# An encoder layer on one core: first loads in another order and smaller pieces, five tiles projected unscaled, a tied operand in the gate/up stage, and the last tile in two column halves

## The chip, the core and the metric

The kernel runs on one core of a Trainium2 chip. Its engines are TensorE (PE; weight loads are listed apart as PEld), VectorE (DVE), ScalarE (ACT), GpSimd (POOL) and SyncE (SP), which issues most loads. The metric is the device time of one execution in microseconds.

## What is computed

One encoder layer over 1280 tokens (a prompt of 256 and a sample of 1024) of width 1024, in float32:

```python
def encoder_layer(x, ...):
    h = rmsnorm(x, attn_norm_g)
    proj = h @ w_in                     # 384 q latents, 256 kv latents, 32 rotary, 3*512 for NA
    a = mla_group(proj[..., :o1], proj[..., o1:o2], proj[..., o2:o3], ...)
    b = na_group(proj[..., o3:], na_rpb)
    mix = jnp.concatenate([rmsnorm(a, mla_out_g), rmsnorm(b, na_out_g)], axis=-1)
    x = x + mix @ w_o
    h2 = rmsnorm(x, ffn_norm_g)
    x = x + (jax.nn.silu(h2 @ w_gate) * (h2 @ w_up)) @ w_down
    return x
# then y = rmsnorm(x, final_norm_g)
```

`mla_group` normalises the latents, rotates the 32 rotary columns and attends over all tokens; `na_group` attends over a window of the token grid.

## The kernel before, in words

**Products.** Every operand is split into a high part (a cast to fp32r) and a low part (the difference); `mm3` (L108) makes three matmuls, L110 to L112, for each 128-row slice: high times high, high times low, low times high. ACT makes the casts; DVE or POOL makes the differences. The tokens are ten tiles of 128 (`NT`), the width eight slices of 128 (`KC`).

**Order.** Tile, the framework, puts every engine's instructions in order with a planner that simulates a timeline and prefers what stands earlier in the program; SP alone keeps the program's order (`manual_schedule`). `tc.issue_after(ins)` puts what is traced inside behind `ins` on its engine. A tile of a pool with `bufs=n` waits until the tile n allocations earlier was used for the last time.

**Latents (L120 to L296).** `w_c` (1024 x 672) is loaded in eight slices, `load_wc` (L138), and scaled by the gain when it is split (`split_g`). x comes twice: transposed as `x_T`, for the products, and by tokens as `x_tm`, for the sum of squares (`rms_x`, L158: a Square on ACT, then two steps on POOL, `rstd_of`). For the first `NU` = 3 tiles x is split as it is loaded, in halves of four slices, between the weight slices; their latents are scaled by the row's factor when they leave PSUM, and x is scaled and split again afterwards (`scale_x`, L167), since the later products read the scaled x in `hT_h`, `hT_l`. `scale_x` spreads the factor to a 128 x 128 tile `r_m` on POOL, lays it across by a product `rr` on PE (bank from the pool `px`), multiplies on DVE (L173) and splits (L152, L153). For tiles 3 to 9 `norm_tile` (L176) does all this ahead of the latents, traced three tiles ahead.

`latents(t)` (L182) sums two PSUM banks `lat` (384 and 288 columns, four banks in rotation) over the eight slices, takes them out (L198 to L203), normalises, and transposes them in two groups through the bank `trc` (L223, L226, L227) into `stg`. `rope_q(t)` multiplies `stg` by `wr` into the bank `pr` (loaded by `load_wr` in three pieces through the buffers of the last weight slices), rotates, and transposes again (L260). In between PE has the first q and k products for the neighbourhood attention, `qk_ftile` (L310), in column chunks of 256, 512 and 512; `HOLD` (L130) puts a chunk behind a step of a tile: step 0 and 1 are the two transpose groups, 2 the rope transposes. Then V is projected with `w_v`, whose buffers lie where the latent stage's were.

**Gate/up (L898 to L1077).** The two FFN input products are made by a scheme of seven sub-products `m` for each pair of 128-column weight blocks; S[m] is an activation operand (sums of quarters `R["11"]` to `R["22"]`), `operand(A, m)` (L892) forms the weight operand: block sums on POOL (`sum_A`, L890), then a cast on ACT (L879) and a difference on POOL (L880) into the ring `wc` of six. For the first pair (`fp` = 0) the order is written out: products 1 and 2 of gate and of up, then 6, 7, 4, 5, 3. Product 6 is the third. Its S6 is built in five token slices from `T2[0..4]`, some of which lie in the buffers `sum` and `A21` that the sums of `operand(.., 6)` need. `differences` (L860) finishes R["12"] and R["21"] for the last two tiles on DVE.

**Down and tail (L1081 to L1233).** The second FFN product is again seven sub-products over eleven steps; m = 7 is last, and its last five steps are made tile by tile for five tiles. After each tile `put` adds PSUM to x (L1143), `final_half` (L1164) takes the Square of the left 512 columns, adds the right half's sum (`prepare`, made earlier), forms the factor in three POOL steps (L1170, L89, L91), scales the left half on DVE and the right half on ACT, and stores both.

## Time and profile before

| | us |
|---|---|
| median of 3 runs | 1632.9 (1630.91 to 1635.21) |
| the profiled execution, its own time | 1632.26 |
| its span | 1630.4 |
| PE busy in it | 1589.9 (98%) |
| DVE, ACT, POOL busy | 884.4 (54%), 715.6 (44%), 663.0 (41%) |
| mean granted clock of TensorE | 0.992 |

Line numbers are those of the kernel before. A group of instructions or a wait is given with the engine, the line and "written tile <- read tiles". "PEclk" or clock is the share of full speed that TensorE was granted: 1.00 is 2.4 GHz, 0.50 is 1.2 GHz. Matmuls are pipelined, so a record's duration is longer than the distance from one start to the next.

### The profile page before, as it was taken

What the parts mean: (1) busy time and instruction counts of PE and PEld (TensorE: products, weight loads), DVE (VectorE), ACT (ScalarE), POOL (GpSimd) and SP (SyncE); (2) the same over time, 40 slices, a digit from 0 to 9 for tenths busy, and PEclk for the clock granted to TensorE, in tenths of its full rate; (3) what the DMA queues carried; (4) which work ended last, traced back from release to release, by engine and by line L of the source; (5) the groups of instructions that cost most, each with busy time, mean ns of one, the idle gap of its engine ahead of it and who ended that gap; (6) DMA issues with size and microseconds to landing.
All of it is one profiled execution on the core that took longest, in us unless ns stands there. A gap on an engine that the chain in (4) does not pass through costs nothing.

```text
span 1630.4 us, 25683 instructions
## 1 busy us (share of the span) xinstructions
PE 1589.9 (98%) x9601; PEld 1447.9 (89%) x9601; DVE 884.4 (54%) x1473; ACT 715.6 (44%) x1478; POOL 663.0 (41%) x823
## 2 busy tenths in 40 slices
PE   7998999999999999999989999999999999999998
PEld 7997889998888888888889999999999998888886
DVE  4654035456777777533374444344444346886676
ACT  5534145455677777644353222333232233443334
POOL 3451425544111119324677656656655651010002
PEclk9999999999999999999999999999999999999999
DMA  6635312234001021234312332222322237843434
GB/s 220 215 101 150 61 39 51 48 107 163 21 18 35 21 94 33 69 108 151 136 33 92 105 109 67 77 94 90 109 99 77 77 120 264 298 140 96 155 102 153
DMA packets 123244, 171.10 MB, mean 105 GB/s; under 512 B 35504, under 2 KB 67120, under 8 KB 123120
## 3 DMA queue, kind: packets, MB, share of 16 engines
q1 hardware_dynamic: 78880, 120.30, 24.1%
q10 hardware_dynamic: 43680, 46.87, 8.3%
q0 software_dynamic: 560, 2.29, 0.3%
q8 instruction: 75, 1.23, 0.3%
q14 instruction: 49, 0.40, 0.1%
HBM read 118.96 MB, written 50.46 MB: 104 GB/s over the span
## 4 chain that ended last, share of the span: by engine, by line
PE 89%; issue 2%; DMA 2%; POOL 2%; ACT 2%; DVE 2%; SPq 0%; ACTq 0%; POOLq 0%; DVEq 0%
PE M L112 11%; PE M L110 11%; PE M L111 11%; PE d L112 5%; PE d L111 5%; PE d L110 5%; PE o L698 4%; PE tp L688 3%; PE po L110 2%; PE po L111 2%; PE pj L110 2%; PE po L112 2%; PE pj L112 2%; PE pj L111 2%; PE na_o L469 2%
## 5 line engine op out<-in xcount | busy, mean ns | idle before, releaser
L111 PE MATMUL M<-S,wc 128*128 128x320 f32 x1056 | 324.3, 309 | 0.0
L110 PE MATMUL M<-S,wc 128*128 128x320 f32 x1056 | 321.9, 309 | 0.0
L112 PE MATMUL M<-S,wc 128*128 128x320 f32 x1056 | 313.0, 310 | 4.1 <-POOL wc L880 4.1
L112 PEld LDWEIGHTS M<-S,wc 128*128 128x128 f32 x1056 | 195.4, 188 | 4.6 <-POOL wc L880 4.6
L111 PEld LDWEIGHTS M<-S,wc 128*128 128x128 f32 x1056 | 198.7, 188 | 0.0
L110 PEld LDWEIGHTS M<-S,wc 128*128 128x128 f32 x1056 | 197.9, 188 | 0.8 <-ACT wc L879 0.3
L880 POOL TENSOR_TENSOR wc<-A,wc 128x512 fp32r<-128x512 f32 x86 | 120.9, 1408 | 83.9 <-ACT wc L879 83.8
L962 DVE TENSOR_TENSOR z<-M,z 128x320 f32<-128x320 f32 x120 | 56.9, 488 | 134.2 <-PE M L112 121.7
L879 ACT CAST wc<-A 128x512 fp32r<-128x512 f32 x86 | 53.5, 622 | 162.2 <-PE M L111 146.3
L880 POOL TENSOR_TENSOR wc<-sum,wc 128x512 fp32r<-128x512 f32 x62 | 88.8, 1433 | 85.5 <-ACT wc L879 81.3
L111 PE MATMUL d<-S,S 128*128 128x512 f32 x310 | 120.7, 390 | 0.0
L112 PE MATMUL d<-S,S 128*128 128x512 f32 x310 | 120.2, 390 | 0.0
L110 PE MATMUL d<-S,S 128*128 128x512 f32 x310 | 119.9, 389 | 0.0
L962 DVE TENSOR_TENSOR zB<-M,zB 128x320 f32<-128x320 f32 x100 | 47.6, 488 | 132.8 <-PE M L112 111.0
L100 DVE TENSOR_TENSOR PT<-tp,PT 128x512 fp32r<-128x512 f32 (+1 forms) x144 | 93.0, 658 | 38.6 <-ACT PT L99 37.5
L879 ACT CAST wc<-sum 128x512 fp32r<-128x512 f32 x62 | 38.4, 619 | 144.4 <-PE M L111 99.1
L99 ACT CAST PT<-tp 128x512 fp32r<-128x512 f32 (+1 forms) x144 | 79.3, 565 | 38.3 <-PE tp L688 34.8
L680 DVE TENSOR_REDUCE mm<-S 128x1 f32<-128x1024 f32 (+1 forms) x80 | 84.8, 1061 | 10.9 <-PE S L112 9.3
L1006 ACT CAST S<-as 128x640 fp32r<-128x640 f32 x58 | 42.3, 729 | 94.4 <-issue 58.6
L682 ACT ACTIVATE ex<-S,mm 128x1024 f32<-128x1024 f32 (+1 forms) x80 | 79.7, 996 | 8.3 <-DVE mm L680 7.7
L711 POOL TENSOR_TENSOR ob<-ob 128x128 f32<-128x128 f32 x40 | 18.3, 457 | 156.9 <-ACT ob L708 153.7
L698 PE MATMUL o<-PT,v 128*128 128x256 f32 x544 | 80.6, 287 | 1.0 <-ACT PT L99 1.0
(404 smaller groups left out, 4113.3 us busy)
## 6 DMA issues: line engine op xcount, KB each, us to landing
as<-act_d SPq DMA_DIRECT2D x73, 320.0 KB
w<-in_w_down_dram SPq DMA_DIRECT2D x44, 256.0 KB
act_d<-z ACTq DMA_DIRECT2D x35, 320.0 KB
act_d<-zB ACTq DMA_DIRECT2D x35, 320.0 KB
A<-in_w_gate_dram SPq DMA_DIRECT2D x42, 256.0 KB
A<-in_w_up_dram SPq DMA_DIRECT2D x42, 256.0 KB
x<-in_x_tm_dram SPq DMA_DIRECT2D x20, 512.0 KB
cT_d<-stg ACTq DMA_DIRECT2D x20, 320.0 KB
```

The lines of the kernel that those rows point to most:

```text
L99: i = nc.scalar.copy(out=hi, in_=ps)
L100: nc.vector.tensor_sub(out=lo, in0=ps, in1=hi)
L110: nc.tensor.matmul(out, lhsT=sh, rhs=mh, start=first, stop=False, **kw)
L111: nc.tensor.matmul(out, lhsT=sh, rhs=ml, start=False, stop=False, **kw)
L112: return nc.tensor.matmul(out, lhsT=sl, rhs=mh, start=False, stop=last, **kw).ins
L680: nc.vector.reduce_max(out=nm[:, u:u + 1], in_=S, axis=AX.X, negate=True)
L682: nc.scalar.activation(ex, S, AF.Exp, bias=nm[:, u:u + 1], scale=1.0, accum_out=l[:, u:u + 1])
L688: nc.tensor.transpose(tp[:, j], ex[:, kt * P:(kt + 1) * P], ident)
L698: nc.tensor.matmul(oT, lhsT=vv, rhs=pt[s][g][:, j], start=kt == 0 and s == 0, stop=kt == nkt - 1 and s == 1)
L879: i0 = nc.scalar.copy(out=hi, in_=raw)
L880: i1 = nc.gpsimd.tensor_tensor(out=lo, in0=raw, in1=hi, op=ALU.subtract)
L962: nc.vector.tensor_add(out=o, in0=ps, in1=a)
```

## The change

- First loads: the gain vector first; x of tiles 0 and 1 in pieces of two, two and four slices between the weight slices; the first weight slice in two column pieces (384, 288), each split by itself; tile 2 after all weights. The last weight slice is loaded into `wqk_raw` and not into the ring of two.
- `NU` = 5: tiles 3 and 4 are loaded, split unscaled and projected like the first three, and scaled afterwards. Tiles 5 to 9 are loaded five tiles ahead and normalised three ahead. `w_qr` comes in one load and one split. `r_m` has two buffers, `rr` one bank instead of two, and the second transpose group has a bank of its own from `px` up to tile 6; the last tile takes banks of `lat` for its transposes and its rope product. `HOLD` names other steps for three chunks.
- Gate/up, first pair: the operand of product 6 for gate is traced before product 1 of up; the last slice of S6 is built behind its cast, and what remains of `differences` behind that slice; only the difference that reads `T2[3]` stays ahead. The operand for up is tied behind the gate operand's low half.
- Tail: for the last tile the last five steps of m = 7 are made for 256 columns and then for the other 256, with an add, a Square and a POOL step for each; the mean's factor and EPS go into `prepare`, and the factor takes one POOL step less. The right half of the last but one tile follows the last tile's last Square.

```diff
@@ -126,9 +126,9 @@
     ck = ra.tile([P, NT, RD], F32, name="ck")
     sk = ra.tile([P, NT, RD], F32, name="sk")
     wr = ra.tile([P, 2, 3, 256], F32R, name="wr")
-    wc, step = [], {}
-    HOLD = {(0, 768): (7, 2), (1, 0): (8, 2), (1, 256): (9, 0), (1, 768): (9, 1)}
-    NU = 3
+    wc, step, rrs = [], {}, {}
+    HOLD = {(0, 768): (7, 2), (1, 0): (9, 0), (1, 256): (8, 2), (1, 768): (9, 2)}
+    NU = 5
 
...
     def load_wc(kc):
-        nm = ("wqk_raw", "wqk_h", "wqk_l", "wqk_h", "wqk_l")
-        raw = (rb.tile([P, KC, P], F32, name=nm[kc], bufs=1 if kc == 0 else 2)
-               .rearrange("p a b -> p (a b)")[:, 0:CW] if kc < 5 else
+        nm = {0: "wqk_raw", 1: "wqk_h", 2: "wqk_l", 3: "wqk_h", 4: "wqk_l", 7: "wqk_raw"}.get(kc)
+        raw = (rb.tile([P, KC, P], F32, name=nm, bufs=1 if nm == "wqk_raw" else 2)
+               .rearrange("p a b -> p (a b)")[:, 0:CW] if nm else
                rx.tile([P, CW], F32, name="wc_raw", bufs=2))
-        load(raw, w_c[kc])
         h = ra.tile([P, CW], F32R, name=f"wc_h{kc}")
         l = ra.tile([P, CW], F32R, name=f"wc_l{kc}")
-        split_g(h, l, raw, kc)
+        cuts = (slice(0, QR), slice(QR, CW)) if kc == 0 else (slice(0, CW),)
+        for cs in cuts:
+            load(raw[:, cs], w_c[kc][:, cs])
+        for cs in cuts:
+            split_g(h[:, cs], l[:, cs], raw[:, cs], kc)
         wc.append((h, l))
 
-    def split_x(t, xT, q=None):
-        ks = slice(0, KC) if q is None else slice(4 * q, 4 * q + 4)
+    def split_x(t, xT, ks=slice(0, KC)):
         sl = (slice(None), ks, slice(t * P, (t + 1) * P))
         nc.scalar.copy(out=hT_h[sl], in_=xT[:, ks])
         nc.vector.tensor_sub(out=hT_l[sl], in0=xT[:, ks], in1=hT_h[sl])
 
-    def load_half(t, xT, q):
-        load(xT[:, 4 * q:4 * q + 4], x_T[t, :, 4 * q:4 * q + 4])
-
-    def rms_x(t):
+    def load_part(t, a, b):
+        load(xu[t][:, a:b], x_T[t, :, a:b])
+        split_x(t, xu[t], slice(a, b))
+
+    def load_x(t):
         x = rx.tile([P, D], F32, name="x", bufs=2)
         load(x, x_tm[t * P:(t + 1) * P, :])
+        return x
+
+    def rms_x(x):
         ss = ra.tile([P, 1], F32, name="ssx", bufs=2)
         nc.scalar.activation(x, x, AF.Square, accum_out=ss)
         r = ra.tile([P, 1], F32, name="rx", bufs=4)
@@ -165,24 +171,26 @@
         return r
 
     def scale_x(t, xT, r):
-        rm = ra.tile([P, P], F32, name="r_m", bufs=1)
+        rm = ra.tile([P, P], F32, name="r_m", bufs=2)
         nc.gpsimd.tensor_scalar(out=rm, in0=ones, scalar1=r, scalar2=1.0, op0=ALU.mult,
                                 op1=ALU.mult)
-        rr = px.tile([P, P], F32, name="rr", bufs=2)
-        nc.tensor.matmul(rr, lhsT=rm, rhs=ident, start=True, stop=True)
+        rr = px.tile([P, P], F32, name="rr")
+        rrs[t] = nc.tensor.matmul(rr, lhsT=rm, rhs=ident, start=True, stop=True).ins
         nc.vector.tensor_mul(out=xT, in0=xT, in1=rr.unsqueeze(1).to_broadcast([P, KC, P]))
         split_x(t, xT)
 
-    def norm_tile(t):
-        xT = (rb.tile([P, KC, P], F32, name="wqk_h", bufs=2) if t in (3, 4) else
-              rx.tile([P, KC, P], F32, name="xT", bufs=3))
+    def load_tile(t):
+        xT = rx.tile([P, KC, P], F32, name="xT", bufs=3)
         load(xT, x_T[t])
-        scale_x(t, xT, rms_x(t))
+        return xT, load_x(t)
+
+    def norm_tile(t, xT, x):
+        scale_x(t, xT, rms_x(x))
 
     def latents(t, r0=None):
         ts_ = slice(t * P, (t + 1) * P)
-        pq = pa.tile([P, QR], F32, name="lat", bufs=4)
-        pk = pa.tile([P, QR], F32, name="lat", bufs=4)[:, 0:KVR + RD]
+        pq = pa.tile([P, 512], F32, name="lat", bufs=4)[:, 0:QR]
+        pk = pa.tile([P, 512], F32, name="lat", bufs=4)[:, 0:KVR + RD]
         for kc in range(KC):
             wh, wl = wc[kc]
             f, e = kc == 0, kc == KC - 1
@@ -218,11 +226,13 @@
                                        op0=ALU.mult, op1=ALU.mult)
         nc.gpsimd.tensor_tensor(out=kr, in0=kr, in1=t2, op=ALU.add)
         stg = ra.tile([P, 2, 6, P], F32R, name="stg", bufs=2)
-        tq = pa.tile([P, 4, P], F32, name="trc")
+        last = t == NT - 1
+        tq = pa.tile([P, 4, P], F32, name="lat" if last else "trc", bufs=4 if last else 1)
         for i in range(4):
             step[t, 0] = nc.tensor.transpose(tq[:, i], c[:, i * P:(i + 1) * P], ident).ins
         split_ps(stg[:, 0, 0:4], stg[:, 1, 0:4], tq)
-        tk = pa.tile([P, 4, P], F32, name="trc")
+        tk = (pa if t + 3 >= NT else px).tile([P, 4, P], F32, name="lat" if last else "trc",
+                                              bufs=4 if last else 1)
         nc.tensor.transpose(tk[:, 0], c[:, 4 * P:5 * P], ident)
         step[t, 1] = nc.tensor.transpose(tk[0:RD, 1], c[:, 5 * P:5 * P + RD], ident).ins
         split_ps(stg[:, 0, 4], stg[:, 1, 4], tk[:, 0])
@@ -233,14 +243,15 @@
         return stg
 
     def load_wr():
-        for c in range(3):
-            raw = rx.tile([P, CW], F32, name="wc_raw", bufs=2)[:, 0:256]
-            load(raw, w_qr[:, c])
-            split_w(wr[:, 0, c], wr[:, 1, c], raw)
+        raw = (rb.tile([P, KC, P], F32, name="wqk_raw").rearrange("p a b -> p (a b)")
+               [:, 0:768].rearrange("p (c n) -> p c n", c=3))
+        load(raw, w_qr)
+        split_w(wr[:, 0], wr[:, 1], raw)
 
     def rope_q(t, stg):
         ts_ = slice(t * P, (t + 1) * P)
-        bank = pa.tile([P, 512], F32, name="pr")
+        last = t == NT - 1
+        bank = pa.tile([P, 512], F32, name="lat" if last else "pr", bufs=4 if last else 1)
         pr = bank[:, 0:256]
         for c in range(3):
             mm3(pr, stg[:, 0, c], stg[:, 1, c], wr[:, 0, c], wr[:, 1, c], c == 0, c == 2)
@@ -263,30 +274,39 @@
         for s in range(2):
             store_r(rope_d[:, s, :, ts_].rearrange("g p t -> p g t"), sr[:, s])
 
-    xu = [rx.tile([P, KC, P], F32, name="xT", bufs=3) for _ in range(NU)]
-    load_half(0, xu[0], 0)
+    xu = [rx.tile([P, KC, P], F32, name="xT", bufs=3) for _ in range(3)]
     load(ga, g_attn)
-    split_x(0, xu[0], 0)
-    halves = [(t, q) for t in range(NU) for q in range(2)][1:]
+    load_part(0, 0, 2)
     for kc in range(KC):
         load_wc(kc)
-        if kc < len(halves):
-            t, q = halves[kc]
-            load_half(t, xu[t], q)
-            split_x(t, xu[t], q)
-    ru = [rms_x(t) for t in range(NU)]
-    norm_tile(NU)
+        for part in {0: ((1, 0, 2),), 1: ((0, 2, 4), (1, 2, 4)), 3: ((0, 4, 8), (1, 4, 8))}.get(kc, ()):
+            load_part(*part)
+    load(xu[2], x_T[2])
+    split_x(2, xu[2])
+    ru = [rms_x(load_x(0))]
     load(gq_b[:, 0:QR], g_q.partition_broadcast(P))
     load(gq_b[:, QR:], g_kv.partition_broadcast(P))
-    load(ck, cos_k)
-    load(sk, sin_k)
-    load_wr()
+    ru.append(rms_x(load_x(1)))
+    for t in (3, 4):
+        xu.append(rb.tile([P, KC, P], F32, name="wqk_h", bufs=2))
+        load(xu[t], x_T[t])
+        split_x(t, xu[t])
+        if t == 3:
+            load(ck, cos_k)
+            load(sk, sin_k)
+            ru.append(rms_x(load_x(2)))
+            load_wr()
+            ru.append(rms_x(load_x(3)))
+    ru.append(rms_x(load_x(4)))
+    ready = {}
     for t in range(NT):
-        if NU < t + 3 < NT:
-            norm_tile(t + 3)
+        if NU <= t + 3 < NT:
+            norm_tile(t + 3, *ready[t + 3])
         stg = latents(t, ru[t] if t < NU else None)
         if t < NU:
             scale_x(t, xu[t], ru[t])
+        if t + 5 < NT:
+            ready[t + 5] = load_tile(t + 5)
         if t + 3 == NT:
             rx.release()
             px.release()
@@ -995,12 +1015,15 @@
         S[m] = [pl.tile([P, 4, NQ], F32R, name=nm, bufs=2) for x in "hl"]
         cuts = [(slice(n * P, (n + 1) * P), T2[n]) for n in range(5)] if m == 6 else [
             (slice(s * NS, (s + 1) * NS), None) for s in range(2)]
-        for cs, from_ in cuts:
-            with ExitStack() as es:
-                for ins in after:
-                    es.enter_context(tc.issue_after(ins))
-                after = split_S(m, cs, from_)
+        for cs, from_ in cuts[:-1] if m == 6 else cuts:
+            after = split_after(m, cs, from_, after)
         return after
+
+    def split_after(m, cs, from_, after):
+        with ExitStack() as es:
+            for ins in after:
+                es.enter_context(tc.issue_after(ins))
+            return split_S(m, cs, from_)
...
@@ -1027,9 +1050,10 @@
             split_f(w_ring[f], raw)
             ops[5, f] = a_ring[f], w_ring[f]
 
-    with tc.issue_after(build_S(6, ())[1]):
-        for t in (NT - 2, NT - 1):
-            differences(nc.vector, t)
+    s6 = build_S(6, ())
+    with tc.issue_after(s6[1]):
+        cs8 = slice(3 * P, 4 * P)
+        difference(nc.vector, R["21"][:, :, cs8], R["21"][:, :, cs8], T2[3])
     for fp in range(NF // 2):
         zp, zn = (rB, "zB") if fp % 2 else (l4[1], "z")
         G, U = C = [zp.tile([P, 2, NTOK], F32, name=zn, bufs=2) for _ in range(2)]
@@ -1047,13 +1071,18 @@
                 if (i, m) == (1, 1):
                     w0[2, 1] = operand(A0[1], 2)
                     A0[1]["12"] = load_A(1, 0, "12", at[5])
-                if (i, m) == (1, 2):
                     w6 = [operand(A0[0], 6, at[6], "A21")]
                     hold = w6[0][2]
+                    s6 = split_after(6, slice(4 * P, 5 * P), T2[4], (hold, s6[1]))
+                    with tc.issue_after(s6[1]):
+                        difference(nc.vector, R["12"][:, :, cs8], R["22"][:, :, cs8],
+                                   R["12"][:, :, cs8])
+                        differences(nc.vector, NT - 1)
                 for s in range(2):
                     with tc.issue_after(last_mm):
                         product(C[i], w0[m, i], m, s, held[i], 0, hold)
-            w6.append(operand(A0[1], 6, at[7], "A22"))
+            with tc.issue_after(w6[0][3]):
+                w6.append(operand(A0[1], 6, at[7], "A22"))
             for n, m in enumerate(SEQ[2:]):
                 w = w6 if m == 6 else [operand(A0[i], m) for i in range(2)]
                 if m != 3:
@@ -1159,18 +1188,27 @@
     def prepare(n, junk):
         x, half = xs[n], halves[:, n:n + 1]
         nc.scalar.activation(junk, x[:, 512:], AF.Square, accum_out=half)
+        nc.vector.tensor_scalar(out=half, in0=half, scalar1=1.0 / D, scalar2=EPS,
+                                op0=ALU.mult, op1=ALU.add)
         nc.gpsimd.tensor_tensor(out=x[:, 512:], in0=x[:, 512:], in1=gl_b[:, 512:], op=ALU.mult)
 
-    def final_half(n):
+    def final_half(n, ps, cuts):
         x, half = xs[n], halves[:, n:n + 1]
         yo = l5r.tile([P, 2, 512], F32, name=f"w1_{n}").rearrange("p a b -> p (a b)")
-        ss = r5a.tile([P, 1], F32, name="ssy", bufs=3)
+        ss = r5a.tile([P, 2], F32, name="ssz", bufs=3)
         r = r5a.tile([P, 1], F32, name="ry", bufs=3)
-        nc.scalar.activation(yo[:, 0:512], x[:, 0:512], AF.Square, accum_out=ss)
-        nc.gpsimd.tensor_tensor(out=ss, in0=ss, in1=half, op=ALU.add)
-        rstd_of(r, ss, D)
+        for j, cs in enumerate(cuts):
+            nc.vector.tensor_add(out=x[:, cs], in0=ps[:, cs], in1=x[:, cs])
+            sq = nc.scalar.activation(yo[:, cs], x[:, cs], AF.Square, accum_out=ss[:, j:j + 1]).ins
+            nc.gpsimd.tensor_scalar(out=ss[:, j:j + 1], in0=ss[:, j:j + 1], scalar1=1.0 / D,
+                                    scalar2=ss[:, j - 1:j] if j else half,
+                                    op0=ALU.mult, op1=ALU.add)
+        nc.gpsimd.tensor_tensor(out=r, in0=ss[:, j:j + 1], in1=mhalf[:, 0:1], op=ALU.pow)
         nc.vector.scalar_tensor_tensor(out=yo[:, 0:512], in0=x[:, 0:512], scalar=r,
                                        in1=gl_b[:, 0:512], op0=ALU.mult, op1=ALU.mult)
+        return sq, (n, yo, x, r)
+
+    def right_half(n, yo, x, r):
         nc.scalar.activation(yo[:, 512:], x[:, 512:], AF.Copy, scale=r)
         load(y[n * P:(n + 1) * P, 0:512], yo[:, 0:512])
         store(y[n * P:(n + 1) * P, 512:], yo[:, 512:])
@@ -1219,17 +1257,26 @@
         group = range(NH - NLAST, NH) if m == 7 and f == NH - 1 else (f,)
         for t in range(5):
             ts_ = slice(t * P, (t + 1) * P)
-            for g in group:
-                h, w = ops[m, g]
-                mm3(ps[t], h[:, 0, ts_], h[:, 1, ts_], w[:, 0], w[:, 1], g == 0, g == NH - 1)
-            if f == NH - 1:
+            cuts = [slice(0, 256), slice(256, 512)] if m == 7 and t == 4 else [slice(0, 512)]
+            for cs in cuts if f == NH - 1 else [slice(0, 512)]:
+                for g in group:
+                    h, w = ops[m, g]
+                    mm3(ps[t][:, cs], h[:, 0, ts_], h[:, 1, ts_], w[:, 0, cs], w[:, 1, cs],
+                        g == 0, g == NH - 1, len(cuts) == 2)
+            if f == NH - 1 and m != 7:
                 put(m, t, ps[t])
                 if m == 3:
                     prepare(t, ps[t])
                 elif m == 4:
                     final(5 + t)
-                elif m == 7:
-                    final_half(t)
+            elif f == NH - 1:
+                sq, args = final_half(t, ps[t], cuts)
+                if t == 4:
+                    with tc.issue_after(sq):
+                        right_half(*prev)
+                if t != 3:
+                    right_half(*args)
+                prev = args
```

## Rows read from the trace of the kernel before

**Rows 1.** Waits of PE: line, releaser: us in total, times, longest

```profile
PE lat L110 <- ACT wc_h L134: 6.9, 1, 6.9
PE M L112 <- POOL wc L880: 4.1, 2, 3.3
PE rr L172 <- POOL r_m L169: 3.6, 4, 1.3
...
PE trc L226 <- DVE stg L100: 1.1, 2, 0.7
```

**Rows 2.** Busy time by stretch: us, PE, PEld, DVE, ACT, POOL, PEclk, DMA, GB/s

```profile
7.00:32.00 25.00, 24.96 (x145) 24.04 (x146) 12.25 (x17) 16.08 (x30) 4.54 (x13) 1.00 0.74 261
32.00:36.00 4.00, 1.39 (x10) 0.94 (x8) 2.36 (x3) 1.00 (x2) 3.84 (x13) 0.97 0.00 0
36.00:46.00 10.00, 9.39 (x32) 8.39 (x33) 7.80 (x13) 4.84 (x11) 8.51 (x17) 0.50 0.59 185
...
120.00:128.00 8.00, 5.34 (x32) 3.94 (x31) 5.76 (x13) 4.12 (x11) 2.36 (x7) 1.00 0.43 119
...
152.00:154.00 2.00, 0.55 (x2) 0.30 (x2) 1.25 (x2) 1.96 (x5) 0.45 (x2) 1.00 0.00 0
154.00:160.00 6.00, 5.95 (x19) 4.63 (x19) 5.61 (x9) 4.98 (x9) 0.00 (x0) 0.72 0.67 203
...
828.00:831.00 3.00, 2.91 (x11) 2.91 (x12) 0.00 (x0) 1.68 (x2) 3.00 (x4) 0.50 0.00 0
```

**Rows 3.** Timeline of SP and ACT, first 20 us: start, us, engine, line, operation

```profile
1.63 0.42 SPq L64 DMA_DIRECT2D wqk_raw<-in_w_c_dram  x1
3.46 0.62 ACT L152 CAST hT_h<-xT 128x512 fp32r<-128x512 f32 x1 [1.45 <-DMA xT<-in_x_T_dram]
6.04 0.85 ACT L134 ACTIVATE wc_h<-wqk_raw,ga 128x672 fp32r<-128x672 f32 x1 [1.97 <-DMA wqk_raw<-in_w_c_dram]
```

**Rows 4.** Busy time by stretch, 8 to 12 us

```profile
8.00:12.00 4.00, 4.00 (x15) 4.00 (x16) 3.48 (x5) 3.62 (x6) 0.00 (x0) 1.00 1.03 388
```

**Rows 5.** Timeline, tile 3 from its Square to its scaled low half

```profile
29.46 1.06 ACT L162 ACTIVATE x<-x 128x1024 f32<-128x1024 f32 x1 [0.49 <-DMA x<-in_x_tm_dram]
...
33.80 0.49 PE L172 MATMUL rr<-ident,r_m 128*128 128x128 f32 x2 [1.17 <-POOL r_m L169]
...
39.89 1.22 DVE L153 TENSOR_TENSOR hT_l<-wqk_h,hT_h 128x1024 fp32r<-128x1024 f32 x1
```

**Rows 6.** Timeline at the third gate/up product: POOL and PE

```profile
823.49 1.66 POOL L890 TENSOR_TENSOR sum<-S 128x512 f32<-128x512 f32 x1 [3.21 <-DVE zB L858]
...
826.78 1.26 POOL L880 TENSOR_TENSOR wc<-S,wc 128x512 fp32r<-128x512 f32 x1
...
828.09 0.64 PE L112 MATMUL M<-S,wc 128*128 128x320 f32 x1 [3.30 <-POOL wc L880]
```

**Rows 7.** Timeline of the last tile's end: add, Square, right half

```profile
1622.27 0.69 DVE L1143 TENSOR_TENSOR x<-d,x 128x512 f32<-128x512 f32 x1 [1.01 <-PE d L112]
...
1623.67 0.61 ACT L1169 ACTIVATE w<-x 128x512 f32<-128x512 f32 x1
...
1625.59 0.72 ACT L1174 ACTIVATE w<-x,ry 128x512 f32<-128x512 f32 x1 [1.21 <-POOL ry L91]
```

**Rows 8.** Timeline: a PSUM operation on DVE and a Square, each of 256 columns

```profile
27.81 0.42 ACT L208 ACTIVATE junk<-c 128x256 f32<-128x256 f32 x1
...
41.22 0.42 DVE L252 TENSOR_TENSOR qr<-pr,ck 128x256 f32<-128x256 f32 x1
```

**Rows 9.** Timeline of PE: products of 256 columns, and of 512 at the end

```profile
136.01 0.28 PE L111 MATMUL pj<-hT_l,wqk_h 128*128 128x256 f32 x1
136.13 0.28 PE L112 MATMUL pj<-hT_h,wqk_l 128*128 128x256 f32 x1
...
1621.61 0.39 PE L111 MATMUL d<-S,S 128*128 128x512 f32 x1
1621.84 0.39 PE L112 MATMUL d<-S,S 128*128 128x512 f32 x1
```

## The prediction

> **What bounds the kernel now.** I read the waits of TensorE first [rows 1]. Its matmuls fill 98% of the span, so the only time to be had lies where they stop or where they run at the lower of the clock's two levels. The wait list says where they stop: the very first product waits 6.9 us for the cast of the first weights, two waits of 4.1 us in all stand at the gate/up start, four of 3.6 us are for the row scales r_m, and two of 1.1 us are for the bank of the transposes. Next I read the stretches [rows 2], because a wait costs more than itself where the clock falls after it. In each row the span minus PE busy is idle time, and a granted clock of 0.50 is the 1.2 GHz level. From 32 to 36 us 2.6 us are idle; from 36 to 46 another 0.6 are idle and the 9.4 busy ones run at 0.50, which throws away half of them, 4.7. The stretch 120 to 128 has 2.7 idle. The start of the V product (152 to 154) has 1.45 idle, and the six microseconds after it run at a mean clock of 0.72, which loses 0.28 of 5.95, or 1.7. At 828 to 831, right after the gate/up wait, 2.9 us run at 0.50 and lose 1.45. The other engines' totals (DVE 54%, ACT 44%, POOL 41%) say that none of them is the bound over the span; they matter through the order in which they take things up.
>
> **Start of the first product.** Before, the queue carries 256 KB of x, the small gain vector and 336 KB of weights before the first product can be fed; the weights are issued at 1.63 us, their cast starts at 6.04 and takes 0.85 [rows 3]. After, it is the gain, 128 KB of x and 192 KB of weights: 324 KB instead of 596. The x half of 256 KB let its cast start at 3.46, the 336 KB behind it landed some 2.5 us later, so 272 KB fewer are worth up to 2.0 us at that pace. Against this stands the gain vector, now ahead of x, which puts the x issue back by 0.44; and a load as large as the old x half needed 2.7 us from issue to cast, so weights issued at 1.63 can hardly be cast before 4.4. I take 1.3 for the landing and 0.3 for the shorter cast (384 of 672 columns of 0.85 us): **1.6 us**, between 0 (the pieces land no earlier) and 2.3.
>
> After that the rate of the loads must hold. Two tiles instead of three take up each slice of weights, so per slice less x is fetched, and SP need not wait with the last slice, which goes to a buffer that is free. Between 8 and 12 us the queue moved 388 GB/s [rows 4]; at that rate 336 KB take 0.9 us, and two tiles of products take some 2 us per slice (25 us of products for three tiles and eight slices is 1.04 per tile and slice). So the loads stay ahead.
>
> The Trainium skill, DMA: Bandwidth & Descriptors, section Bandwidth, speaks against smaller pieces: it asks for loads of 1 MiB for three quarters of the peak. The row of 8 to 12 us disagrees, 388 GB/s with loads of 256 and 336 KB, several in flight. The same page's section on the anatomy of one DMA gives 2.0 us plus the bytes at 436 GB/s; by that the old weights would have landed at 5.0 us, not near 6.0, and 272 KB fewer would be worth an estimated 0.6 us, so this term would be 0.9 in place of 1.6.
>
> **Tiles 3 and 4 unscaled.** The hole at 32 to 46 us has its reason in [rows 5]: tile 3's latents need its x scaled first. Its sum of squares starts at 29.46, its r_m product is at 33.80, and the low half of its scaled x is written from 39.89 to 41.1, 11.7 us from one end to the other, while the three unscaled tiles end by 32. After, tiles 3 and 4 need only a load, a cast and a subtraction; the scale enters at the eviction, as for the first three. Tile 3's x is the last of 6.2 MB on the queue, which at the 261 GB/s of 7 to 32 us [rows 2] is there by about 27 us, ahead of the 31 us at which tile 2 will end; tile 4's is 2.3 MB behind it, at about 36, ahead of 38. So there are two tiles, some 15 us of products, where the hole was, and what is removed is 2.6 + 0.6 + 4.7 = 7.9 us. The price is that both are cast twice, two casts of 1.05 and two subtractions of 1.2 more; ACT (4.8 of 10 us busy at 36 to 46) covers its part, DVE (7.8 of 10) just. If that cover is gone, DVE delays an eviction by at most these 2.4 us. I take **7.0 us** of the 7.9; bounds 2 (half the hole comes back at tile 5) and 7.9.
>
> **Later in that stage.** The other r_m waits are 3.6 − 1.2 = 2.4 us [rows 1]. Tiles 5 to 9 are loaded five ahead instead of three, and r_m has two buffers; but rr has one bank instead of two. I take **1.0**, bounds −1 and 2.4. The second transpose group gets its own bank (taken from rr) up to tile 6, and the last tile uses the four latent banks; the bank waits are 1.1 us [rows 1] of the 2.7 idle in 120 to 128. The reordered holds move the 512-column K chunk to the eighth tile and put the short one before the last rope product, so what they cover changes places. **1.0**, bounds −1.5 and 2.7. The last chunk now comes behind the last rope transposes, so the buffers that the V weights need come free earlier relative to the products; of 1.45 + 1.7 = 3.1 us I take **1.0**, since the chain load, cast, product is itself several microseconds long; bounds −1 and 3.1.
>
> **Third gate/up product.** In [rows 6] POOL's subtraction for the low half of its weights runs only at 826.78, because two block sums stand ahead of it, the first of which waits until 823.49 for DVE to free a buffer. PE, which ran out at 824.8, waits 3.3 us. After, the operand is traced one product earlier, its cast goes ahead of the last slice of S6, the buffer is freed by the one difference that reads it, and the other operand is queued behind the low half. POOL is free at 820.3 (3.2 before 823.49), so the low half can be done by 822 and PE goes on. Then the second operand: one sum for the first operand, two sums and the low half for the second, 1.7 + 1.7 + 1.3 + 1.3 us and a 0.6 cast from 822, is 828.6, and PE asks for it at about 824.8 + 24 × 0.147 = 828.3. So the second wait (4.1 − 3.3 = 0.8) stays in part. Behind the moved slice on DVE stand the three differences and S7's casts; PE takes S7 7 us after S6, and they sum to about 5. Of 4.1 + 1.45 = 5.5 us I take **4.0**, bounds 0 and 5.5. The new tie can also cost: the copies of the product before now wait for that cast on ACT.
>
> **Tail.** In [rows 7] the last tile's add starts at 1622.27, its square only at 1623.67 because ACT has the previous tile's right half, and its scaled output ends at 1626.3 and is then stored. After, the left 256 columns are done before the products end: then 0.42 (add) [rows 8], 0.1, 0.51 (square with its read), two steps on POOL of the three that took 1.21 together, some 0.95, and 0.72, which from 1622.27 is 1625.0, or 1.3 earlier. Thirty half-width products follow each other at 0.12 [rows 9], as long as fifteen at 0.23. If both halves share a bank in such a way that the first add must wait for the last product, the chain is one add and one square longer than that, and 0.5 to 0.9 stays. The stores of the last two tiles come closer together. **1.1**, bounds 0.5 and 1.4.
>
> **The sum.** 1.6 + 7.0 + 1.0 + 1.0 + 1.0 + 4.0 + 1.1 = 16.7 us. The profiled execution took 1632.26, so 1615.6; the median of the runs is 0.6 above it, so about **1616 us**. All upper bounds give 25.3, that is 1607.6.
>
> **Rivals.**
> A. The hole moves to tile 5, the first that must be scaled: its load waits for tile 0's buffer, and its chain is as long as tile 3's was. For it: DVE and POOL were both over 75% busy when this happened before. Against: PE gets to tile 5 only at about 45 us plus the small products of five tiles, the chain can start with tile 0's scaling at about 30. Then the four early terms after the first fall away: 1.6 + 4.0 + 1.1 = 6.7, **1626**.
> B. The gate/up wait only changes its place, from the first operand to the second or to the copies tied behind the cast: 12.7, **1620**.
> C. The orders written down bind nothing, because the planner's choice elsewhere gives back what they win: **1632**.
> D. Slower. Each tile's load is queued behind the scaling of the tile that had its buffer. If that is placed late, PE stops for the whole 11.7 us chain [rows 5] and runs on at half clock (4.7 lost), 16.4 per occurrence. Then only 1.6 + 7.9 + 4.0 + 1.1 = 14.6 stand against it: once is 1634.7, twice 1651. It decides from the point at which tile 5's square starts later than about 45 us; **1640**. Against it: r_m of tile 0 was late before because tile 3's scaling stood ahead of it, and now nothing does.
>
> **Chances.** Forecast 0.58, B 0.16, A 0.13, C 0.07, D 0.06. Range 1607 to 1629: it takes in all upper bounds, B and A, and leaves out C and D. Under 0.3% (4.9 us) is what a measurement of this kernel can't tell from no change; faster than 1628 are the forecast, B and nearly all of A: 0.86; same 0.08; slower 0.06.
>
> **What would show it.** First product near 5.3 us; no idle and a granted clock of 1.00 from 30 to 50 us; no wait of M for POOL's wc over 1 us near 810 and a clock of 1.00 after it; the last scaled output finished some 2.8 us after the last product (4.1 before). The prediction is wrong if a stretch of half clock stands elsewhere before 60 us, or if the planner's new order opens waits in stages that the diff doesn't touch.

## The result and the profile after

The changed kernel takes 1619.2 us (median of six, 1617.07 to 1620.38) beside 1631.91 for the kernel before: a ratio of 0.992, with an interval of 0.9907 to 0.9933. The profiled execution took 1617.07, its span is 1615.2; the median is 2 us longer, which the last section comes back to.

The waits of TensorE after (line, releaser: us in total, times, longest), which answer to [rows 1]:

```profile
PE lat L110 <- ACT wc_h L134: 5.2, 1, 5.2
...
PE pr L271 <- POOL qr L268: 2.6, 3, 1.3
PE lat L110 <- ACT stg L99: 2.2, 1, 2.2
PE trc L232 <- DVE c L224: 1.6, 1, 1.6
...
PE M L110 <- ACT S L892: 1.2, 1, 1.2
PE M L110 <- ACT wc L899: 1.1, 2, 0.9
...
PE rr L178 <- POOL r_m L175: 0.9, 1, 0.9
PE pr L110 <- DVE sr L105: 0.9, 1, 0.9
```

The first product comes 1.7 us earlier, the waits for r_m have gone from 3.6 to 0.9, and the 4.1 of the gate/up start are now 2.1 behind other releasers. New are a wait of 1.6 for scaled latents (c) and one of 2.2 for a cast (stg). The three waits for the rope sums (qr) are not new; before, they were

```profile
PE pr L260 <- POOL qr L257: 2.5, 3, 0.9
```

but only one of those lay ahead of 100 us, and now all three do. The stretches say when. Of before (busy time of PE, PEld, DVE, ACT, POOL, then PEclk, DMA share, GB/s):

```profile
30.00:46.00 16.00, 12.77 (x53) 10.92 (x52) 11.18 (x17) 6.85 (x16) 13.38 (x31) 0.68 0.44 140
46.00:100.00 54.00, 50.40 (x345) 48.89 (x344) 36.35 (x55) 25.48 (x56) 32.27 (x55) 1.00 0.60 189
100.00:153.50 53.50, 48.49 (x294) 42.63 (x291) 23.61 (x58) 19.87 (x53) 12.66 (x37) 1.00 0.45 124
```

and the same stretches of after, with two shorter ones:

```profile
30.00:46.00 16.00, 14.93 (x102) 14.30 (x101) 10.23 (x19) 10.56 (x23) 13.17 (x27) 1.00 0.63 197
46.00:100.00 54.00, 49.48 (x336) 47.03 (x335) 40.08 (x65) 24.06 (x60) 34.04 (x62) 1.00 0.59 173
100.00:145.00 45.00, 41.81 (x233) 36.13 (x232) 18.87 (x46) 16.07 (x38) 7.44 (x20) 0.92 0.43 120
120.00:126.00 6.00, 6.00 (x16) 4.92 (x17) 2.17 (x5) 1.35 (x4) 0.00 (x0) 0.51 0.62 164
808.00:815.00 7.00, 4.89 (x22) 4.22 (x20) 6.12 (x5) 2.21 (x5) 6.92 (x5) 0.78 0.12 37
```

In each row, length minus PE busy is idle time, and length times (1 − PEclk) is what the lower clock takes, at most (idle time under the lower clock counts in both). The hole of 30 to 46 cost 3.2 + 16 × 0.32 = 8.3 us and costs 1.1. But 46 to 100 has gone from 3.6 to 4.5 idle, and 100 to the first V product (at 153.5 before, at 145.1 after) has 3.2 idle and 45 × 0.08 = 3.6 of lower clock, most of it at 120 to 126. Before, that part had 5.0 idle, and 1.7 of lower clock right behind it [rows 2].

The gate/up start after, in the timeline (start, us, engine, line, operation; in brackets the idle time before it), which answers to [rows 6]:

```profile
808.66 0.42 ACT L980 COPY z<-M 128x320 f32<-128x320 f32 x1 [0.89 <-PE M L112]
808.98 0.62 ACT L899 CAST wc<-S 128x512 fp32r<-128x512 f32 x1
809.26 1.48 DVE L878 TENSOR_TENSOR A<-zB,zA 128x512 f32<-128x512 f32 x1 [0.20 <-ACT z L980]
...
809.65 0.41 PE L110 MATMUL M<-S,wc 128*128 128x320 f32 x1 [0.89 <-ACT wc L899]
...
810.15 1.71 POOL L900 TENSOR_TENSOR wc<-S,wc 128x512 fp32r<-128x512 f32 x1
810.77 0.62 ACT L892 CAST S<-A 128x512 fp32r<-128x512 f32 x1 [1.17 <-DVE A L878]
...
811.44 0.41 PE L110 MATMUL M<-S,wc 128*128 128x320 f32 x1 [1.23 <-ACT S L892]
```

The wait for GpSimd's low half is gone. In its place stand two: the cast of the weights behind a copy that waits for PE, and the last slice of S, whose difference runs on VectorE only at 809.26.

The end after, which answers to [rows 7]:

```profile
1607.48 0.28 PE L112 MATMUL d<-S,S 128*128 128x256 f32 x1
1607.80 0.75 DVE L1201 TENSOR_TENSOR x<-d,x 128x256 f32<-128x256 f32 x2 [1.58 <-PE d L112]
...
1610.47 0.72 ACT L1212 ACTIVATE w<-x,ry 128x512 f32<-128x512 f32 x1 [0.69 <-POOL ry L1206]
```

Both half additions start behind the last product; the last scaled output ends 3.4 us after it (4.1 before).

### The profile page after: what moved, and what is told of

The parts are those of the page before. It is cut to its first block, busy times and chain, and to the rows that moved or that the text cites. A ratio compares the mean times of both kernels' runs of the same rounds, so it can differ in the third digit from the quotient of the medians.

```text
span 1615.2 us, 25739 instructions
## 1 busy us (share of the span) xinstructions
PE 1582.2 (98%) x9616; PEld 1444.1 (89%) x9616; DVE 891.1 (55%) x1483; ACT 715.5 (44%) x1484; POOL 664.7 (41%) x815
## 4 chain that ended last, share of the span: by engine, by line
PE 88%; DVE 3%; issue 2%; ACT 2%; POOL 2%; DMA 1%; ACTq 0%; SPq 0%; POOLq 0%; DVEq 0%
PE M L110 11%; PE M L112 11%; PE M L111 11%; PE d L111 5%; PE d L110 5%; PE d L112 5%; PE o L718 4%; PE tp L708 3%; PE na_o L489 2%; PE po L110 2%; PE po L111 2%; PE po L112 2%; PE pj L110 2%; PE pj L111 2%; PE pj L112 2%
## 5 line engine op out<-in xcount | busy, mean ns | idle before, releaser
L111 PE MATMUL d<-S,S 128*128 128x512 f32 (+1 forms) x314 | 121.2, 386 | 0.0
L112 PE MATMUL d<-S,S 128*128 128x512 f32 (+1 forms) x314 | 120.7, 386 | 0.0
L110 PE MATMUL d<-S,S 128*128 128x512 f32 (+1 forms) x314 | 120.4, 387 | 0.0
```

Source lines behind the costliest of these rows:

```text
L110: nc.tensor.matmul(out, lhsT=sh, rhs=mh, start=first, stop=False, **kw)
L111: nc.tensor.matmul(out, lhsT=sh, rhs=ml, start=False, stop=False, **kw)
L112: return nc.tensor.matmul(out, lhsT=sl, rhs=mh, start=False, stop=last, **kw).ins
```

## Experiments

In the expectations, "the start of the attention" is the first V product.

**The three parts alone.** Each is the kernel before with one part of the diff; beside them the changed kernel again.

> The kernel before with the edits of the latents stage alone (load order and pieces, five unscaled tiles, orders by hand, banks); gate/up and tail as before. Terms of the prediction for this part: 1.6 + 7.0 + 1.0 + 1.0 + 1.0 = 11.6 us, so about 1620.3 beside a median of 1631.9. Reading of the two profiles: first product 1.7 earlier, stretch 32 to 46 us 6.8 better, waits of 52 to 96 us 0.9 worse, stretch 114 to 136 us 2.7 worse, v stage 3.1 better and 2 us from an earlier end of the half clock at the start: 10 us, so about 1622. If the later parts of the change were what brought most of it, less than 6 us.

> The kernel before with the edits of the gate/up stage alone (last slice of S for product 6, its differences and the cast of the second weight tied to the casts of the first). Terms of the prediction: 4.0 us, about 1627.9 beside 1631.9. Reading of the two profiles: 5.5 us lost to waits and half clock before, 3.8 after, so 1.7 us, about 1630.2. If the wait only changes place at full cost: no change, 1631.9.

> The kernel before with the edits of the last output tile alone (two column halves, sums on POOL, right half of the tile before it later). Terms of the prediction: 1.1 us, about 1630.8 beside 1631.9; in the profile the last scaled output about 2.8 us after the last product. Reading of the two profiles: first addition does not start before the last product ends, 3.4 us after it, so 0.8 us.

> The changed kernel itself, beside the three parts, for its spread from run to run: 1617 to 1621. If the parts add up, the three differences from the kernel before sum to this one's, about 12.7 us; if the planner's order of one part undoes another, they do not.

| kernel | median us | ratio to before, interval |
|---|---|---|
| latents alone | 1627.55 | 0.9963 (0.995 to 0.9977) |
| gate/up alone | 1631.93 | 0.9986 (0.9978 to 0.9995) |
| tail alone | 1630.42 | 0.9981 (0.997 to 0.9991) |
| all three | 1621.51 | 0.993 (0.9918 to 0.9943) |

Times 1634.2, the median of before beside them, the parts are 6.0 + 2.3 + 3.1 = 11.4 us, and the whole is 11.4. The intervals of the parts are 1.4 to 2.2 us wide to either side, so they add up to within some 3 us; that both sums are the same to a tenth is luck. Their sizes are not those of my terms. In the profiles the gate/up edit alone gives 1.5 us (first gate/up product to the 300th), and the tail's edit 2.0 from the first down product on. The latents part is 10.8 us ahead where the attention scores begin in its one profile, which is its fastest run (1621.16), and only 6.0 by the median. Three of its other four runs had a mean granted clock of 0.991 where this one had 0.994, which is some 5 us of 1625; where they lost it is not seen.

**Three unscaled tiles in place of five**, all else as in the change:

```diff
-    NU = 5
+    NU = 3
...
-        split_x(t, xu[t])      # t = 3, 4
...
+    ready = {3: (xu[3], x3), 4: (xu[4], load_x(4))}
```

> The changed kernel, but with three unscaled tiles instead of five; its first loads, pieces, hand-written orders and banks stay. If the five unscaled tiles are what closed the hole of 32 to 46 us (the prediction's term of 7.0, read as 6.8 in the changed kernel's profile), PE waits for the scaled halves of tiles 3 and 4 again: 5 to 8 us of idle time and half clock between 30 and 50 us, median near 1627 beside 1619 to 1621. If the new order of the first loads was enough, under 2 us, median near 1621.

1612.75 us, a ratio of 0.9873 (0.986 to 0.9887). I had expected a loss; it is some 7 us faster than the change and the best kernel of the study. Its stretches:

```profile
30.00:46.00 16.00, 13.15 (x72) 11.90 (x71) 12.05 (x22) 7.63 (x17) 8.72 (x19) 0.79 0.51 153
46.00:100.00 54.00, 53.67 (x375) 53.28 (x374) 34.91 (x62) 27.72 (x66) 34.46 (x69) 1.00 0.63 191
100.00:137.50 37.50, 37.50 (x223) 33.18 (x222) 19.18 (x44) 15.16 (x36) 7.22 (x20) 1.00 0.48 139
```

The hole is back as expected: 2.9 idle and 16 × 0.21 = 3.4 of lower clock, 6.2 where five tiles have 1.1. But behind it there is nearly nothing: 0.3 us idle and no lower clock up to the first V product, at 137.5. Five tiles buy 5 us in the hole and pay 4.5 + 3.2 + 3.6 = 11 later; of these the 3.6 of lower clock did not come in every execution (last section).

**Four unscaled tiles.**

```diff
-    NU = 5
+    NU = 4
...
+    ready = {4: (xu[4], load_x(4))}
```

> The changed kernel with four unscaled tiles (0 to 3); tile 4 is scaled before it is used. With five, attention starts at 145.1, with three at 137.5. If each tile scaled a second time costs its share later, it starts near 141, with a wait for tile 4 alone near 40 us (1 to 3 us) and waits of about 2 us in 46 to 100 us: median near 1616. If the losses of the changed kernel come from an order that the planner happens to find with five, there is no such middle: either near 138 or near 145 and later.

1613.77 us, 0.9879 (0.9864 to 0.9894), which the intervals don't tell apart from three tiles. Attention starts at 139.1, between my two cases.

```profile
30.00:46.00 16.00, 14.77 (x98) 13.37 (x96) 9.54 (x19) 9.03 (x25) 11.58 (x29) 1.00 0.57 167
46.00:100.00 54.00, 51.59 (x352) 49.85 (x351) 37.65 (x68) 25.72 (x59) 31.55 (x62) 1.00 0.61 183
100.00:139.00 39.00, 37.21 (x223) 32.68 (x222) 18.29 (x42) 15.44 (x37) 6.68 (x19) 1.00 0.50 142
```

Four close the hole as well as five do (1.2), and lose 2.4 + 1.8 later. So idle time behind the hole grows with the number of unscaled tiles: 0.3, 4.2, 7.7 (the next expectation has 3.3 for four tiles; the rows give 4.2). That fitted the idea that the second scaling and splitting is what costs.

**Tiles 3 and 4 never scaled**, with five unscaled tiles:

```diff
-        if t < NU:
+        if t < 3:
             scale_x(t, xu[t], ru[t])
```

> The changed kernel (five unscaled tiles) without the scaling of tiles 3 and 4 after their latents: their factor on GpSimd and PE, the multiply on VectorE and the second splitting on ScalarE and VectorE are left out, so their q, k and v come from unscaled rows. Idle time of PE from 46 us to the start of the attention stage was 7.7 us with five unscaled tiles, 3.3 with four, 0.4 with three. If it is the deferred scaling that makes it, the idle time falls to about 0.4 to 2 us with the hole still closed: attention starts near 132 to 136, median near 1608 to 1611. If it is the order that the planner finds with five, waits of 4 us or more stay in 52 to 126 us and attention starts at 140 or later.

1618.22 us, 0.9914 (0.99 to 0.9928), although it leaves out two multiplies, two casts and two subtractions.

```profile
30.00:46.00 16.00, 14.92 (x101) 14.32 (x101) 10.23 (x19) 10.56 (x23) 13.15 (x27) 1.00 0.64 198
46.00:100.00 54.00, 50.09 (x346) 48.46 (x345) 35.73 (x62) 22.24 (x59) 32.82 (x60) 1.00 0.60 173
100.00:141.50 41.50, 38.35 (x217) 32.96 (x216) 18.97 (x46) 15.98 (x38) 7.44 (x20) 0.96 0.47 131
```

VectorE is down from 40.1 to 35.7 us of 54, near what it has with three tiles (34.9), and PE still idles 3.9 + 3.2; attention starts at 141.6. Waits of the same kinds stand there: 2.2 for stg at the same place, 2.1 for c (at 75 us in place of 87) and 1.1 for qr. So the losses don't need the deferred scaling; that idea fell as the main cause. The removal is not a clean one, though: leaving the work out changed the planner's order too, chiefly between 55 and 90 us, so this kernel does not show that the scaling costs nothing in the change's own order.

**The q and k weights split later**, in the change:

```diff
+            if i < 2:
+                es.enter_context(tc.issue_after(rrs[NT - 1]))
...
             nc.gpsimd.tensor_tensor(out=raw, in0=raw, op=ALU.mult,
```

> The changed kernel (five unscaled tiles) with GpSimd's splitting of the first q and k weights tied behind the last tile's transposed factor (rr of tile 9, 76.8 us), which puts it where it lay with three unscaled tiles (77.6 us; 64.8 us in the changed kernel). If that early splitting is what slows the tiles' sums on GpSimd and VectorE, the waits of 70 to 88 us (3.9 us) and with them the late places of 114 to 126 us go: attention starts near 138 to 140 in place of 145.1, median near 1612 to 1615. If the second scaling and splitting of tiles 3 and 4 between 46 and 77 us is the cause, it stays within 1.5 us of 145.1. If neither load but only the planner's order makes the losses, any other order can come, of either sign, with no tie to GpSimd's times.

1620.13 us, 0.9916 (0.9902 to 0.9931). The timeline says that the edit did nothing: GpSimd starts on the weights at 64.82 and 77.89, as in the change (64.77 and 77.85). The instruction named is PE's, and the tie orders within one engine. Whether that splitting costs is thus not tested. The kernel serves as a further execution of the change's order: up to the first V product PE, VectorE, ScalarE and GpSimd take their work in the same sequence as in the change. It idles 4.6 + 3.2 us at the same places, and this time there is no lower clock at all between 100 and the first V product, at 142.6. In the five profiles with this sequence (the change twice, the latents alone, the slice first, and this one) the first V product comes at 142.6 to 146.4; in the two with three tiles, which share a sequence of their own, at 137.5 and 138.1.

**The hand-written orders of before**, in the change:

```diff
-    HOLD = {(0, 768): (7, 2), (1, 0): (9, 0), (1, 256): (8, 2), (1, 768): (9, 2)}
+    HOLD = {(0, 768): (7, 2), (1, 0): (8, 2), (1, 256): (9, 0), (1, 768): (9, 1)}
```

> The changed kernel with the four hand-written orders of the kernel before for the chunks of the first q and k products. The changed kernel loses 3.2 us idle and 2.9 us to half clock between 114 and 126 us. If the new orders made that (no chunk left to fill the place), most of it goes here: start of the attention 3 to 6 us earlier than 145.1, median near 1616. If ScalarE's queue of stores makes it, the idle time of 2 us before the last tile's rope product and the half clock stay: within 1.5 us of the changed kernel.

1619.61 us, 0.9919 (0.9905 to 0.9932): no difference. Attention starts at 146.5, and the 3.2 us of idle time behind 100 and the wait of 2.2 stay, so the new orders don't make them.

**Stores of tiles 7 to 9 on GpSimd's queue** in place of ScalarE's:

```diff
...
+        if t < 7:
+            store_r(out, in_)
+        else:
+            store_p(out.bitcast(F32), in_.bitcast(F32))
...
```

> The changed kernel with the stores of latents, rope keys and rope queries of the tiles 7, 8 and 9 issued by GpSimd in place of ScalarE. If the seven issues (about 3 us in ScalarE's queue between 115.7 and 119.3 us) hold the cast that PE waits for at 117.8 to 120.0, the cast runs near 116, the wait of 2.2 us goes and the granted clock stays at 1.00: up to 5 us, attention starts near 140 to 142, median near 1615. If the wait comes from the order on PE, it stays: within 1 us. A third way: GpSimd's own issues delay its sums for the rope queries, and another wait of about the same size comes.

The place in the timeline of the change (ACTq is ScalarE issuing a transfer):

```profile
117.93 1.32 ACTq L73 DMA_DIRECT2D kr_d<-stg  x2
...
119.36 0.75 ACT L99 CAST stg<-lat 128x512 fp32r<-128x512 f32 x2 [1.80 <-DVE qr L266]
...
120.00 0.58 PE L110 MATMUL lat<-wr,stg 128*128 128x256 f32 x1 [2.20 <-ACT stg L99]
```

and in the timeline of this kernel:

```profile
118.68 0.75 ACT L99 CAST stg<-lat 128x512 fp32r<-128x512 f32 x2 [0.72 <-PE pr L112]
...
119.32 0.48 PE L110 MATMUL lat<-wr,stg 128*128 128x256 f32 x1 [0.68 <-ACT stg L99]
```

ScalarE issues two transfers for 1.3 us, and the cast runs as soon as they are out. Without them the wait is 0.7 in place of 2.2 and the idle time behind 100 is 1.6 in place of 3.2. So ScalarE's queue makes that half; what is left is 0.7 for sr, which holds the bank of the rope product, and 0.7 for the cast. The rest of the expectation failed: the clock fell behind these shorter waits as well (0.96 over 100 to 144), attention starts at 144.0, and the whole doesn't show the gain: 1621.82 us, 0.9931 (0.9916 to 0.9945).

**The slice of S first.** The ninth tile's difference goes behind the last slice of S for product 6:

```diff
-    with tc.issue_after(s6[1]):
-        difference(nc.vector, R["21"][:, :, cs8], R["21"][:, :, cs8], T2[3])
...
                     with tc.issue_after(s6[1]):
+                        difference(nc.vector, R["21"][:, :, cs8], R["21"][:, :, cs8], T2[3])
```

> The changed kernel with the difference of block 21 of the ninth tile put behind the last slice of S for product 6, as the other differences are, so that VectorE starts the tenth tile's multiply at about 805.9 in place of 807.3 (1.79 us of that difference stand ahead of it). If that slice is what product 6 waits for (1.23 us at 810.2 to 811.4), the slice comes 1.4 to 1.7 us earlier, the wait goes, and with it perhaps the 1.7 us of half clock: 1.2 to 2.9 us less between the first gate/up product and its 300th, which takes 49.2 us. If GpSimd's low part of the weights (done at 811.86) is as late, a wait for it takes its place: under 0.5 us.

1621.88 us, 0.9931 (0.9918 to 0.9943), and the stage takes 51.8 us in place of 49.2. Its waits for M in the list of waits:

```profile
PE M L112 <- POOL wc L900: 3.6, 1, 3.6
...
PE M L110 <- ACT wc L899: 2.0, 2, 1.1
```

The slice does come earlier and nothing waits for it. But the 3.6 us stand 10 us further on, at the second operand. GpSimd's next sum needs the buffer that the ninth tile's difference reads, and now has to wait until that difference has run behind the slice; GpSimd's subtraction for the second operand then takes 2.5 us in place of 1.3. Counted from the first gate/up product, that low half is done 1.5 us later than in the change, and PE asks for it 2.8 us sooner:

```profile
814.65 1.67 POOL L910 TENSOR_TENSOR sum<-S 128x512 f32<-128x512 f32 x1 [1.24 <-DVE zB L878]
...
823.52 0.63 PE L112 MATMUL M<-S,wc 128*128 128x320 f32 x1 [3.61 <-POOL wc L900]
```

Neither case of my expectation is this: both looked at the first operand alone. Instead of a gain, 2.6 us are lost.

**Joined**: three unscaled tiles, a bank of its own for the last tile's second column half, and product 6's operands cast and summed earlier. Of the edit, the two further parts:

```diff
+                late = pd.tile([P, 512], F32, name="d", bufs=8)
+                nc.vector.tensor_add(out=xl, in0=ps[t][:, 256:], in1=xl)
...
+                    at = late if len(cuts) == 2 and f == NH - 1 and cs.start else ps[t]
...
-                if (i, m) == (1, 1):
+                if (i, m) == (0, 2):
                     w0[2, 1] = operand(A0[1], 2)
...
                     w6 = [operand(A0[0], 6, at[6], "A21")]
                     hold = w6[0][2]
```

> Three unscaled tiles with the change's other edits, and two further ones that stages of their own show. Last output tile: the second column half in a bank of its own, so that the first half's addition does not wait for the last product; the last scaled output 2.6 to 2.9 us after the last product in place of 3.4 us (0.5 to 0.8 less). Gate/up: product 6's first weight is cast ahead of the copies of product 2, its fourth sum comes behind its low part, and the ninth tile's difference behind the last slice: if the order on ScalarE, GpSimd and VectorE is what the two waits of 0.9 and 1.2 us come from, they shrink to about 1 us together, 1 to 2.8 us less between the first product and the 300th (49.2 to 49.5 us now); if the sums on GpSimd bound it, a wait for the low part of 1 us or more takes their place. Median 1609 to 1612, beside 1612.75 with three unscaled tiles alone.

1615.62 us, 0.9888 (0.9873 to 0.9902), not faster than three tiles alone. The tail does what was expected: the first half's addition runs at 1604.82, ahead of the last product (1605.65 to 1605.93), and the last output is scaled 2.9 us after that. VectorE's timeline:

```profile
1604.82 0.41 DVE L1202 TENSOR_TENSOR x<-d,x 128x256 f32<-128x256 f32 x1
1605.97 0.42 DVE L1202 TENSOR_TENSOR x<-d,x 128x256 f32<-128x256 f32 x1 [0.73 <-PE d L112]
...
1608.08 0.75 DVE L1208 SCALAR_TENSOR_TENSOR w<-x,ry,gl_b 128x512 f32<-128x512 f32 x1 [0.80 <-POOL ry L1207]
```

The gate/up stage does not: 51.2 us, its waits 1.9 for the cast, now of the second operand, and 1.7 for three others. Two attempts to order this place by hand have only moved the wait from the first operand to the second.

## Why the prediction was right, and where it was not

The time (1616 forecast, 1619.2 measured) and the sign hold, but partly by luck, since errors of the terms cancel. In the profiles:

| step | term | measured |
|---|---|---|
| first product | 1.6 | 1.7 |
| hole of tiles 3 and 4 (30 to 46 us) | 7.0 | 7.3 |
| r_m waits later (46 to 100) | 1.0 | −0.9 |
| bank, holds, V start | 2.0 | about 0 |
| third gate/up product | 4.0 | 1.8 (1.5 alone) |
| tail | 1.1 | 0.7, and 1.3 in the down products |
| not named | 0 | about 2 up to the end of V, 1.4 at 361 to 398 |

**First product.** Right. In the other profiles it comes at 6.1 and 6.7 with the old loads and at 4.9 to 5.3 with the new ones, so the 1.7 is known to some half a microsecond. The Trainium skill, DMA: Bandwidth & Descriptors, section on the anatomy of one DMA, would have made this term an estimated 0.9; the row's pace, 1.6, was nearer to the 1.7 measured. But that section gives its figure for transfers that GpSimd issues, and these loads are SP's, so the comparison is no test of it. One thing the rows hid: up to 11.7 us before and 9.7 us after, products of 384 columns start 0.32 us apart, and later 0.17, so TensorE begins at half pace although PEclk says 1.00 there. The 25 us that I divided by three tiles and eight slices hold some 5 us of it.

**Tiles 3 and 4.** The size in the hole is right. The step that failed is the one that priced its cover: "DVE delays an eviction by at most these 2.4 us". I costed the deferred scaling by its instructions and looked only at the hole: behind it five tiles lose 11 us in these profiles that three don't, 7.4 of them idle time. The net worth of this edit is negative. Of the rivals only D had that, by one stop for a whole chain of scaling; rival A put the loss at tile 5 alone, and it came as small waits from 56 us on. The kernel that leaves the deferred work out still idles 7.1 of the 7.7 us. Nor can it be only that PE reaches the later tiles sooner and waits for what isn't ready: that could give back at most the 5 us won and leave the first V product where it is with three tiles, and it comes 4.5 to 8.9 us later. That the planner's order is the cause follows only from what is left; why it finds this order with five tiles is open.

**Later in that stage.** With three tiles all of this idle time is gone (0.3 us from 46 on, against 3.6 + 5.0), so the other edits reach my upper bounds by themselves. In the change as it stands the waits for r_m behind 46 us are gone as well, all 2.4 us of them, but 1.6 for c and 1.8 more for qr stand in their place, which makes the −0.9; and the second of these steps is eaten by the casts behind ScalarE's stores and the lower clock after them. The V start did come free of a wait (PE is busy for all of 145 to 213.5, at 1.00).

**Gate/up.** Rival B in part. My step "the low half can be done by 822 and PE goes on" left out that ScalarE takes the cast behind a copy that itself waits for PE, and that the last slice hangs on VectorE's queue. The clock also fell again (0.78 in 808 to 815), where I had said that it would not.

**Tail.** The branch that I had named, 0.5 to 0.9 if the first addition must wait for the last product, is what came: 0.7. With a bank of its own for the second half, the first addition ran ahead of the last product: it was the shared tile.

**What would show it.** First product at 5.2 for 5.3; the clock at 1.00 from 30 to 50; no wait of M for GpSimd's wc: right. No idle time there (1.1 us is left) and a clock of 1.00 after the gate/up start (0.78): wrong. The last scaled output 2.8 us after the last product: 3.4. My warning sign, new waits opened by the planner's order, came true, but inside the changed stage and not, as I had written, in stages that the diff doesn't touch.

## What to carry to other kernels

A hole that is closed by deferring work is to be costed up to the end of the stage, not to the end of the hole: where a planner orders the engines, a changed start gives another order for everything behind it, and that can cost more than the hole wins. When an edit has a size (five tiles), run the sizes beside it; three beat five by 7 us, and no reading of the one profile showed it. And look at whether a tie did anything before its time is read.

## What the runs showed of the hardware

The same order of work loses the clock in one execution and not in the next. From 100 us to the first V product the change lost 3.6 us to the lower clock in one profile and 1.7 in its other, and the kernel with the tie that moved nothing lost none, each behind the same wait of 2.2 us. At 360 to 375 us, which the change doesn't touch, two profiles of the changed kernel differ. The execution of 1617.07:

```profile
360.00:375.00 15.00, 13.68 (x104) 12.57 (x103) 10.56 (x33) 9.21 (x26) 2.61 (x9) 1.00 0.70 265
```

and that of 1623.35:

```profile
360.00:375.00 15.00, 12.97 (x74) 12.02 (x73) 8.53 (x26) 8.22 (x20) 2.33 (x8) 0.77 0.81 314
```

The second has 2.0 us idle in place of 1.3 and 15 × 0.23 = 3.5 of lower clock; from the first attention score to the first output product it takes 39.7 us there and 35.0 in the first, 4.7 of the 6.3 us between the two executions. Before took 36.4, so 1.4 of the 15.2 us between its profile and that of after come from here. A term for the clock is therefore a chance, not a sum.

In the three kernels without the tail's edit the first 1,140 down products follow each other at 228.4 ns on average. In eight of the eleven profiles with it they do at 227.3 (in the other three, which have waits in between, at 227.5 to 228.0): 1.3 us, before the first product of half width is reached. The cause is open.
